# A decoder trunk on one core: two units side by side at the head, a pool window as a difference, no diagonals, a tail shared with GpSimd, and sine tables on GpSimd

## The chip, the cores and the metric

The kernel runs on one core of a Trainium2 chip. The metric is the device time of one execution in microseconds (us). Three runs of the kernel before gave 1794.53, 1795.22 and 1798.0 us, median 1795.22.

The engines go by the profile's names: PE is TensorE's matmul stream and PEld its weight load, DVE is VectorE, ACT is ScalarE, POOL is GpSimd, and SP issues most DMAs. Each engine works through its own instructions in the order in which they were written; a wait holds up everything behind it on that engine.

## The reference, cut to what matters

One layer, fp32, 2048 tokens of 1024 channels. Half of the projection `u` goes to a pooling mixer (four groups of 128 channels with windows 2, 4, 8, 16), half to a complex diagonal scan; both are joined by `w_out`, and a SwiGLU FFN with 2816 inner channels follows.

```python
def rmsnorm(x, g):
    y = xf * lax.rsqrt(jnp.mean(xf * xf, axis=-1, keepdims=True) + RMS_EPS)
    return y.astype(x.dtype) * g

# pool_mixer: for each window w
    mean = (c - lagged) / jnp.minimum(n_pos, float(w))[None, :, None]
    diffs.append(mean - ug[:, :, gi])
...
# ssm_mixer
    abar_r = mag * jnp.cos(li * dt)
    abar_i = mag * jnp.sin(li * dt)
    ...
    _, _, s_r, s_i = lax.associative_scan(_complex_affine_combine, (a_r, a_i, bu_r, bu_i), axis=1)
    y = ... + d_skip * ug
    y = jax.nn.gelu(y)
    y = y * jax.nn.sigmoid(y @ w_glu + b_glu)
...
        u = rmsnorm(h, norm_mix[i]) @ w_in[i]
        h = h + jnp.concatenate([y_pool, y_ssm], axis=-1) @ w_out[i]
        h = h + swiglu(rmsnorm(h, norm_ffn[i]), w_gate[i], w_up[i], w_down[i])
    return rmsnorm(h, norm_final)
```

## The kernel before, in words

**Matmuls.** Activations lie with 128 channels on the partitions and tokens along the free axis, in four token blocks of 512. A large fp32 matmul is done as three fp32r products of split operands: hi·hi, hi·lo, lo·hi. `split` (L335) makes the halves: ACT rounds the raw tile to hi (for x with the norm's gain `gmix` as scale), DVE subtracts it from the raw tile and so gets lo. One such product is a 128x512 matmul on PE; a unit of stage A is 24 of them (8 channel tiles times 3) for 128 output channels of one token block. The FFN saves products by a Strassen-like scheme that DVE's additions feed.

**Stages**, by the trace: the head and stage A to about 206 us (`phase_a`, first key 1 with the scan's four weight tiles m = 4 to 7, the token blocks in the order 3, 2, 1, 0; then key 2 with the pool's tiles); the eight lanes of the scan from about 133 to 337 us, PE being filled up beside them with the pool half of `w_out` (its partial sums go out through POOL's queue as `hp` and come back); GLU, the scan half of `w_out` and the second norm to 532 us; the FFN to 1526, its last down projection to 1777, and the tail, in which the last token block is done in two halves of 256 tokens (`c0` = 0 and 256).

**Norms.** Squares of a block are added up over the channel tiles, and a matmul with `mean` (128x1, each 1/1024) puts the means of 512 tokens as four columns into PSUM. `rsqrt_cols` (L358) takes the reciprocal root there in 13 small DVE instructions on the tile `nwt`. `rbank` (L390) makes four diagonal tiles with them (`ident` times a column of `rstd`, on DVE) and multiplies these by a tile of ones on PE, which lays rstd along the free axis over all partitions.

**The head.** `w_load(4)`, the gain vector and the four quarters of x (512 KB each) are loaded first, then w_in tiles 5, 6, 7. The first unit (m = 4) takes the quarters as they come; each `x_split` is followed by the squares of that quarter on ACT and their addition on DVE; tile 5 is split after the fourth quarter.

**Pool units.** `pool_unit` builds the window sum of 2, 4, 8 or 16 tokens by doubling, corrects the first tokens with `pin`, and subtracts w times u with a scalar_tensor_tensor of 1024 columns. There are two halves (1024 tokens each) for each of four windows.

**The scan.** For each lane s of 8, `ssm_table` (L717) forms cosine and sine tables from angle sums with six 128x512 tensor_tensors on DVE; `ssm_lane` then rotates the input, scans it (L886) and rotates it back, some 10 us of DVE. Table s+1 is formed while lane s runs. `ssm_build` clears a tile `T0` (L774, four times). The outputs of two lanes each are stored as `ys` with eight DMAs on POOL's queue.

**Order.** A planner writes the program out: class `Flow` keeps modelled clocks of the engines (`fl.t`, `fl.now`); generators registered as sides are resumed when their modelled inputs are due, or yield at `fl.when(...)`. So an edit to one instruction's engine or duration can shift what others are written before or after it.

**The tail.** Each output group of the last block is squared (ACT), added to one of two running sums (DVE), and the eighth square is given to the mean matmuls directly. When `rsqrt_cols` and `rbank` are through, groups k = 0 to 2 of each half are multiplied by rstd on POOL (`PK`; they were scaled with `gfin` on ACT before), the others on DVE with gfin in one scalar_tensor_tensor; SP stores the pairs.

## Time and profile before

| | |
|---|---|
| median of 3 runs | 1795.22 us (1794.53 to 1798.0) |
| the profiled execution | 1794.41 us, span 1792.5 us |
| PE busy | 1756.9 us, 98% of the span |
| DVE busy | 1343.6 us, 75% |
| ACT busy | 695.7 us, 39% |
| POOL busy | 164.9 us, 9% |
| mean granted TensorE clock | 0.994 |

The profile is of one execution. The span is the time from its first to its last recorded instruction or transfer; the execution's own time is 1.9 us longer. "Busy" counts every engine alone, so the columns overlap; 35.6 us of the span have no matmul. "Idle before" and the releaser after an arrow tell how long an engine stood before a row, and what it waited for last.

### The profile page before, as it was taken

To read this page: it belongs to the slowest core of one execution; us is meant where nothing else is said; L and a number is where in the kernel's file an instruction comes from. 1 tells how busy PE (TensorE), PEld (TensorE's weight loads), DVE (VectorE), ACT (ScalarE), POOL (GpSimd) and SP (SyncE) were. 2 spreads that over 40 slices of the span, in tenths; PEclk is the share of its full clock that TensorE was granted. 3 is DMA by queue.
4 is the path that set the end of the run, shared out by engine and by line. 5 is a ranking of instruction groups with operands and counts; after the bars stand their busy time and mean duration, and the time that the engine had idled before them with its cause. 6 is when DMAs were issued, how large, how long until landed. Compare 5 with 4: busy or idle time off the path is not lost.

```text
span 1792.5 us, 23179 instructions
## 1 busy us (share of the span) xinstructions
PE 1756.9 (98%) x8192; PEld 1441.7 (80%) x8192; DVE 1343.6 (75%) x2319; ACT 695.7 (39%) x1152; POOL 164.9 (9%) x311
## 2 busy tenths in 40 slices
PE   7999999999989999999999999999999999999997
PEld 5878777788868888888888888888888888888886
DVE  7879999657998777787788777776766556666666
ACT  5512223343353333333355333333334445354452
POOL 0000010100000121111101111211100000000001
PEclk9999999999999999999999999999999999999998
DMA  5462434684612255444364343454547665766752
GB/s 183 134 129 76 111 105 109 176 294 172 228 47 100 102 190 191 170 172 171 128 226 169 140 168 124 154 218 148 198 145 250 194 193 198 290 219 198 235 178 105
DMA packets 154596, 301.92 MB, mean 168 GB/s; under 512 B 25520, under 2 KB 49072, under 8 KB 154480
## 3 DMA queue, kind: packets, MB, share of 16 engines
q1 hardware_dynamic: 128912, 214.97, 37.7%
q0 software_dynamic: 25568, 85.48, 12.7%
q8 instruction: 64, 1.05, 0.2%
q14 instruction: 52, 0.43, 0.1%
HBM read 206.40 MB, written 92.80 MB: 167 GB/s over the span
## 4 chain that ended last, share of the span: by engine, by line
PE 89%; DVE 5%; issue 3%; DMA 2%; POOL 0%; ACT 0%; SPq 0%; DVEq 0%; POOLq 0%; ACTq 0%
PE p L207 89%; DVE s L184 3%; DMA s<-in_win_dram 1%; DVE s L195 1%; DVE t L184 1%; POOL ys L222 0%; DMA s<-ys 0%; DMA s<-in_cst_dram 0%; SPq L222 0%; DMA s<-in_wout_dram 0%; DMA ys<-b 0%; ACT s L203 0%; DVE b L184 0%; PE p L211 0%; DVE nwt L184 0%
## 5 line engine op out<-in xcount | busy, mean ns | idle before, releaser
L207 PE MATMUL p<-s,s 128*128 128x512 f32 (+3 forms) x4812 | 1200.9, 383 | 21.6 <-ACT s L203 11.1
L207 PEld LDWEIGHTS p<-s,s 128*128 128x128 f32 (+2 forms) x4812 | 849.1, 183 | 209.8 <-DVE s L184 14.0
L207 PE MATMUL p<-s,t 128*128 128x512 f32 (+2 forms) x1356 | 397.4, 383 | 0.7 <-DVE s L184 0.6
L207 PE MATMUL p<-s,b 128*128 128x512 f32 x1080 | 334.3, 389 | 0.0
L184 DVE TENSOR_TENSOR s<-s,s 128x512 f32<-128x512 f32 (+4 forms) x329 | 277.9, 868 | 64.5 <-ACT s L203 55.2
L207 PEld LDWEIGHTS p<-s,t 128*128 128x128 f32 x1356 | 249.7, 188 | 52.7 <-DVE s L184 1.8
L207 PEld LDWEIGHTS p<-s,b 128*128 128x128 f32 x1080 | 202.7, 188 | 42.0
L203 ACT ACTIVATE s<-s 128x512 fp32r<-128x512 f32 (+3 forms) x199 | 155.2, 792 | 111.5 <-DVE s L184 42.2
L203 ACT ACTIVATE s<-t 128x512 fp32r<-128x512 f32 (+1 forms) x186 | 113.7, 624 | 124.5 <-PE p L207 88.0
L184 DVE TENSOR_TENSOR s<-p,s 128x512 f32<-128x512 f32 (+3 forms) x185 | 116.8, 652 | 46.9 <-PE p L207 45.6
L203 ACT ACTIVATE t<-p 128x512 f32<-128x512 f32 (+1 forms) x107 | 63.5, 594 | 189.1 <-PE p L207 183.5
L203 ACT ACTIVATE t<-s 128x512 f32<-128x512 f32 (+2 forms) x126 | 76.6, 616 | 140.1 <-DVE s L184 112.1
L203 ACT ACTIVATE s<-p 128x512 f32<-128x512 f32 (+2 forms) x98 | 56.2, 590 | 168.5 <-PE p L207 142.1
L184 DVE TENSOR_TENSOR s<-t,s 128x512 fp32r<-128x512 f32 (+2 forms) x145 | 96.9, 678 | 27.4 <-issue 19.0
L207 PE MATMUL p<-b,s 128*128 128x512 f32 (+2 forms) x428 | 115.9, 389 | 0.7 <-DVE s L184 0.7
L184 DVE TENSOR_TENSOR t<-p,t 128x512 f32<-128x512 f32 x117 | 79.5, 688 | 34.4 <-PE p L207 31.9
L222 POOL DMA_DIRECT2D act_P<-t x81 | 43.8, 543 | 528.9 <-DVE t L184 528.4
L207 PEld LDWEIGHTS p<-b,s 128*128 128x128 f32 (+1 forms) x428 | 64.1, 172 | 21.0 <-issue 5.2
L184 DVE TENSOR_TENSOR s<-b,s 128x512 fp32r<-128x512 f32 (+1 forms) x89 | 60.9, 686 | 25.4 <-issue 12.1
L203 ACT ACTIVATE s<-b 128x512 fp32r<-128x512 f32 (+1 forms) x99 | 61.2, 622 | 47.3 <-PE p L207 25.5
L184 DVE TENSOR_TENSOR t<-t,t 128x512 f32<-128x512 f32 (+2 forms) x108 | 73.5, 681 | 5.6 <-ACT t L203 4.5
L184 DVE TENSOR_TENSOR s<-s,t 128x512 f32<-128x512 f32 (+1 forms) x77 | 52.9, 688 | 31.5 <-ACT t L203 30.4
(128 smaller groups left out, 1225.4 us busy)
## 6 DMA issues: line engine op xcount, KB each, us to landing
act_P<-t POOLq DMA_DIRECT2D x81, 256.0 KB, 4.9
s<-in_x_dram SPq DMA_DIRECT2D x40, 512.0 KB, 6.6
t<-ws_P SPq DMA_DIRECT2D x78, 256.0 KB, 2.7
t<-act_P SPq DMA_DIRECT2D x71, 256.0 KB, 3.1
b<-act_P SPq DMA_DIRECT2D x66, 256.0 KB, 3.0
s<-in_wu_dram SPq DMA_DIRECT2D x62, 256.0 KB, 5.3
s<-in_wd_dram SPq DMA_DIRECT2D x50, 256.0 KB, 5.3
t<-in_wd_dram SPq DMA_DIRECT2D x50, 256.0 KB, 3.2
```

What stands on the lines that cost most here:

```text
L184: self.eng(e).tensor_tensor(out, a, b, op=op)
L195: self.eng(e).scalar_tensor_tensor(out=out, in0=a, scalar=s, in1=b, op0=op0, op1=op1)
L203: self.nc.scalar.activation(out=out, in_=a, func=func, **kw)
L207: self.nc.tensor.matmul(out, l, r, start=start, stop=stop, skip_group_check=more)
L222: e.dma_start(dst, src)
```

## The change

Five edits, none of which changes what is computed.

1. Head. The first w_in tile is loaded in two halves with the first quarter of x (in two halves too) between them; tile 5 comes before the third and fourth quarters. `a_pair` does units m = 4 and 5 of the first block side by side, two quarters of one, two of the other, then in turn. Squares of that block are taken after all splits, and tile 6 is split before them.
2. The pool window of 2 is formed as a difference: the mean of two tokens minus the token itself is half of (previous minus this one), so the last subtraction with 1024 columns, and the `pin` correction, fall away for gi = 0.
3. Norms. `rbank` takes the column of rstd, broadcast over 128 columns, as one matmul operand and `ident` as the other; the four diagonals and the tile of ones are gone. EPS is put into PSUM by a matmul of `ident` with a small tile `eps`, and the Newton steps read PSUM, 11 DVE instructions instead of 13.
4. Tail. The first half's eight groups are all multiplied on POOL, of the second half k = 0 to 2 as before. Six squares are added up; the seventh and eighth go to the mean matmuls directly.
5. Scan. The six instructions of each `ssm_table` and the clearing of `T0` go from DVE to POOL.

```diff
@@ -25,6 +25,9 @@
+TE = 'g'
+DN = 6
+FN = 5.0
@@ -44,7 +47,7 @@
-PK = {3: 3, 2: 3}
+PK = {0: range(8), 256: range(3)}
@@ -360,37 +363,37 @@
+        mm(ps[:, js], ident, eps[:, js], True, False, 0.1)
         for i, s1 in enumerate(parts):
-            yield fl.when(s1) + SL
+            while callable(s1):
+                if s1():
+                    s1 = s1()
+                else:
+                    yield fl.now + 0.3
+            yield fl.when(s1) + (SL if c1 - c0 == 512 else 0.1)
...
-                mm(ps[:, j:j + 1], s1[:, j * 128:(j + 1) * 128], mean, i == 0 and j == js.start, i == len(parts) - 1 and j == js.stop - 1, 0.22)
+                mm(ps[:, j:j + 1], s1[:, j * 128:(j + 1) * 128], mean, False, i == len(parts) - 1 and j == js.stop - 1, 0.1)
...
-        a, y, h = (nwt[:, i, 0:n] for i in range(3))
-        ts("v", a, ps[:, js], EPS, None, ADD)
-        PS.free(ps)
-        ts("v", h.bitcast(I32), a.bitcast(I32), 1, None, ALU.logical_shift_right)
-        ts("v", a, a, -0.5, None, MUL)
+        y, h = (nwt[:, i, 0:n] for i in range(2))
+        ts("v", h.bitcast(I32), ps[:, js].bitcast(I32), 1, None, ALU.logical_shift_right)
...
-            tt("v", h, h, a, MUL)
+            stt("v", h, h, -0.5, ps[:, js], MUL, MUL)
...
+        PS.free(ps)
...
     def rbank(idx, c0=0, c1=512):
-        diag = T([128, 4, 128])
...
-        for j in js:
-            ts("v", diag[:, j, :], ident, rstd[:, idx, j:j + 1], None, MUL)
...
-            mm(ps[:, j * 128:(j + 1) * 128], ones, diag[:, j, :], True, True, 0.22)
-        T.free(diag)
+            mm(ps[:, j * 128:(j + 1) * 128], rstd[:, idx, j:j + 1].to_broadcast([128, 128]), ident, True, True, 0.22)
@@ -413,10 +416,12 @@
+        xhl[key, tb, q] = (hi, lo)
+        if key == 1 and not fl.now:
+            return raw
...
-        xhl[key, tb, q] = (hi, lo)
@@ -473,11 +478,33 @@
+    def a_pair(tb, ms, ps, half_way):
+        for n, (u, q) in enumerate(((0, 0), (0, 1), (1, 0), (1, 1), (0, 2), (1, 2), (0, 3), (1, 3))):
+            fl.until(lambda: ms[u] in whl)
+            hi, lo = whl[ms[u]]
+            xh, xl = xhl[1, tb, q]
+            for i in range(2):
+                k = 2 * q + i
+                mm(ps[u], hi[:, k, :], xh[:, i, :], k == 0, False)
+                mm(ps[u], hi[:, k, :], xl[:, i, :], False, False)
+                mm(ps[u], lo[:, k, :], xh[:, i, :], False, k == 7)
+            yield
+            if n == 3:
+                for h in half_way:
+                    h()
+
     def phase_a(key, ms, unit_done, hooks):
...
-            for mi, m in enumerate(ms):
+            units = list(enumerate(ms))
+            if key == 1 and n == 0:
+                ps = bank(), bank()
+                yield from a_pair(tb, ms, ps, hooks.pop((0, 1)))
+                for mi in range(2):
+                    unit_done(n, tb, mi, ps[mi])
+                units = units[2:]
+            for mi, m in units:
@@ -518,9 +545,18 @@
-        if half == 0:
-            tt("v", cur[:, :, 0:2], cur[:, :, 0:2], pin[:, gi], MUL)
-        stt("v", cur, u, -float(w), cur, MUL, ADD)
+        if gi:
+            if half == 0:
+                tt("v", cur[:, :, 0:2], cur[:, :, 0:2], pin[:, gi], MUL)
+            stt("v", cur, u, -float(w), cur, MUL, ADD)
+        else:
+            yield from room(1, 3)
+            cur, hl = S([128, 8, 128]), halo[:, 0, 0, 7:8]
+            tt("v", cur[:, 1:8, :], u[:, 0:7, :], u[:, 1:8, :], SUB)
+            tt("v", cur[:, 0, 1:128], u[:, 7, 0:127], u[:, 0, 1:128], SUB)
+            tt("v", cur[:, 0, 0:1], hl if half else u[:, 0, 0:1], u[:, 0, 0:1], SUB)
+            if half == 0:
+                cp("v", hl, u[:, 7, 127:128])
@@ -721,10 +757,10 @@
-            tt("v", t[:, i].rearrange("p q (m n) -> p q m n", n=16), x, wide(y[:, 1, qs], 3, sh), MUL)
+            tt(TE, t[:, i].rearrange("p q (m n) -> p q m n", n=16), x, wide(y[:, 1, qs], 3, sh), MUL)
...
-        tt("v", tab[:, 0], tab[:, 0], tmp[:, 0], SUB)
-        tt("v", tab[:, 1], tab[:, 1], tmp[:, 1], ADD)
+        tt(TE, tab[:, 0], tab[:, 0], tmp[:, 0], SUB)
+        tt(TE, tab[:, 1], tab[:, 1], tmp[:, 1], ADD)
@@ -771,8 +807,8 @@
-        nc.vector.memset(T0, 0.0)
-        fl.t["v"] += 0.6
+        nc.gpsimd.memset(T0, 0.0)
+        fl.t["g"] = max(fl.t["g"], fl.now) + 1.2
@@ -994,22 +1030,37 @@
-        w_load(4)
+        t0, w4 = ORD[1][0], S([128, 8, 128])
+        xr0 = xraw[1, t0, 0] = S([128, 2, 512])
...
-        for q in range(4):
-            x_load(1, ORD[1][0], q)
-        for m in (5, 6, 7):
+        load(w4[:, 0:4], win[4][:, 0:4, :])
+        for i in range(2):
+            load(xr0[:, i], x4[t0][:, i, :])
+        load(w4[:, 4:8], win[4][:, 4:8, :])
+        x_load(1, t0, 1)
+        w_load(5)
+        for q in (2, 3):
+            x_load(1, t0, q)
+        for m in (6, 7):
...
-        w_split(4, True)
+        whl[4] = (S([128, 8, 128], F32R), S([128, 8, 128], F32R))
+        raws = []
...
-            x_split(1, ORD[1][0], q)
-        st_side[ORD[1][0]] = fl.side(stats_x(ORD[1][0]), None)
-        fl.now += 7.0
-        w_split(5)
-        at(0, 1, w_split, 6)
+            if q < 2:
+                split(w4[:, 4 * q:4 * q + 4], *(t[:, 4 * q:4 * q + 4] for t in whl[4]))
+            elif q == 2:
+                S.free(w4)
+                w_split(5, True)
+            raws.append(x_split(1, t0, q))
+        w_split(6, True)
+        for q in range(4):
+            xacc[t0] = sq_add(xacc.get(t0), raws[q], q == 0)
+            S.free(raws[q])
+        st_side[t0] = fl.side(stats_x(t0), None)
+        fl.now += FN
@@ -1765,20 +1816,23 @@
-            if m < PK[tb]:
+            if not c0 or n <= DN:
...
+            if n > DN:
+                sums.setdefault((tb, c0, "p"), {})[n] = sq
+                return
...
-            elif n < 8:
+            else:
...
-            if n == 8:
-                while sums[tb, c0, "d"] < 8:
+            if n == DN:
+                while sums[tb, c0, "d"] < DN:
...
-                yield from last(tb, c0, c1, sq)
+                yield from last(tb, c0, c1)
...
         def down(hh):
@@ -1891,23 +1946,30 @@
+            mine = [k for k in range(8) if k in PK[c0]]
+
             def pooled():
-                for k in range(PK[tb]):
+                for k in mine:
...
-            for k in range(PK[tb], 8):
+            for k in range(8):
+                if k in mine:
+                    continue
...
-                stt("v", hk, hk, gfin[:, k:k + 1], ps[:, c0:c1], MUL, MUL)
+                if c0 and k >= DN:
+                    stt("v", hk, hk, gfin[:, k:k + 1], ps[:, c0:c1], MUL, MUL)
+                else:
+                    tt("v", hk, ps[:, c0:c1], hk, MUL)
...
-            T.free(r, sq)
+            T.free(r, *more.values())
@@ -1937,8 +1999,8 @@
-        nc.vector.memset(ones, 1.0)
...
+        nc.vector.memset(eps, EPS)
...
```

**Places in the order.** First SP's queue at the head: which loads are issued first. `s_1` is the first w_in tile, `in_x_dram` the quarters of x, each 512 KB at 128x1024. Before:

```order
L222 DMA s_1_338<-in_win_dram 128x1024
L222 DMA vec<-in_vecs_dram 128x64
L222 DMA s_2_341<-in_x_dram 128x1024
L222 DMA s_3_343<-in_x_dram 128x1024
L222 DMA s_4_345<-in_x_dram 128x1024
L222 DMA s_5_347<-in_x_dram 128x1024
L222 DMA s_6_349<-in_win_dram 128x1024
```

And in the changed kernel:

```order
L225 DMA vec<-in_vecs_dram 128x64
L225 DMA s_1_338<-in_win_dram 128x512
L225 DMA s_2_339<-in_x_dram 128x512 x2
L225 DMA s_1_338<-in_win_dram 128x512
L225 DMA s_3_345<-in_x_dram 128x1024
L225 DMA s_4_347<-in_win_dram 128x1024
L225 DMA s_5_349<-in_x_dram 128x1024
L225 DMA s_6_351<-in_x_dram 128x1024
```

The second w_in tile (`s_6_349` before, `s_4_347` after) has moved ahead of the third and fourth quarters of x. On PE the last products of the first unit before (`p_1`) are followed by the second unit (`p_3`), with the mean matmuls (`p_2`) after six of its products:

```order
L207 MATMUL p_1_402<-s_21_391,s_9_360 128x512
L207 MATMUL p_1_402<-s_20_390,s_10_361 128x512
L207 MATMUL p_3_438<-s_11_364,s_23_399 128x512
L207 MATMUL p_3_438<-s_12_365,s_23_399 128x512
L207 MATMUL p_3_438<-s_11_364,s_24_400 128x512
L207 MATMUL p_2_411<-mean,t_1_409 128x1 x4
L207 MATMUL p_3_438<-s_14_372,s_23_399 128x512
```

In the changed kernel `p_1` and `p_2` are the two units, `s_13`/`s_14` the second quarter of x, `s_15`/`s_16` tile 5, `s_17`/`s_18` the third quarter, and `p_3` takes the eps matmul:

```order
L210 MATMUL p_3_421<-eps,ident 128x4
L210 MATMUL p_1_411<-s_13_374,s_9_362 128x512
L210 MATMUL p_1_411<-s_14_375,s_9_362 128x512
...
L210 MATMUL p_1_411<-s_13_374,s_10_363 128x512
L210 MATMUL p_2_412<-s_11_366,s_15_380 128x512
L210 MATMUL p_2_412<-s_12_367,s_15_380 128x512
L210 MATMUL p_2_412<-s_11_366,s_16_381 128x512
```

The second unit's first half now stands after 12 products of the first unit, and needs tile 5 there; the mean matmuls stand behind the first two units and half of the third. On POOL, in the stretch of the last lanes, only stores stood before (`hp` partial sums, `ys_81` the outputs of the lanes 4 and 5):

```order
L222 DMA hp_2_105<-s_232_2757 128x1024
L222 DMA hp_3_106<-s_237_2800 128x1024
L222 DMA hp_0_107<-s_243_2865 128x1024
L222 DMA hp_1_108<-s_247_2934 128x1024
L222 DMA ys_81<-b_3_2219 16x8x256 x8
L222 DMA hp_2_109<-s_256_3017 128x1024
```

There stand now the tables of lane 6 (`s_247`, `s_248`) and lane 7 (`s_255` and on) between them:

```order
L225 DMA hp_2_105<-s_231_2700 128x1024
L225 DMA hp_3_106<-s_235_2738 128x1024
L187 TENSOR_TENSOR s_247_2891<-s_50_703 128x512
L187 TENSOR_TENSOR s_248_2892<-s_50_703 128x512
...
L187 TENSOR_TENSOR s_247_2891<-s_247_2891,s_248_2892 128x512 x2
L225 DMA hp_0_107<-s_244_2845 128x1024
L225 DMA ys_81<-b_3_2200 16x8x256 x8
L187 TENSOR_TENSOR s_255_3000<-s_50_703 128x512
```

So the table of lane 7 stands behind the eight stores of `ys_81`, which themselves wait for the GELU of lane 5's output.

## Rows read from the trace of the kernel before

**Rows 1.** The page's busy times, with the share of the span and the instructions.

```profile
PE 1756.9 (98%) x8192; PEld 1441.7 (80%) x8192; DVE 1343.6 (75%) x2319; ACT 695.7 (39%) x1152; POOL 164.9 (9%) x311
```

**Rows 2.** What PE waited for, over the whole span: engine, line and tile waited for, then us in total, times, longest.

```profile
PE p L207 <- ACT s L203: 11.1, 2, 9.3
PE p L207 <- DVE s L184: 10.8, 9, 3.3
```

**Rows 3.** Busy time by stretch: start:end of the stretch, its length, then busy us (and instructions) of PE, PEld, DVE, ACT, POOL, the granted clock, the DMA engines' share and GB/s.

```profile
142.00:206.00 64.00, 64.00 (x360) 50.63 (x357) 63.25 (x116) 18.47 (x27) 0.00 (x0) 1.00 0.25 84
206.00:302.00 96.00, 94.04 (x604) 72.36 (x600) 91.07 (x151) 26.48 (x46) 13.14 (x24) 1.00 0.50 115
302.00:350.00 48.00, 47.80 (x233) 36.35 (x234) 38.15 (x58) 15.04 (x25) 7.55 (x14) 1.00 0.48 139
360.00:471.00 111.00, 110.94 (x505) 92.36 (x506) 78.29 (x127) 41.80 (x58) 6.25 (x12) 1.00 0.64 228
471.00:532.00 61.00, 54.36 (x222) 42.86 (x221) 58.17 (x75) 28.62 (x42) 2.80 (x6) 0.94 0.33 121
532.00:1526.00 994.00, 994.00 (x4402) 823.52 (x4402) 720.59 (x1149) 394.70 (x675) 121.96 (x226) 1.00 0.49 169
```

**Rows 4.** The head in order of time (start, us, engine, line, operation, tiles, shape, count, and in brackets the idle time before it and its releaser). The row of 18 matmuls ends where the window was cut, at 27 us, with the second unit's last product.

```profile
8.48 1.34 ACT L203 ACTIVATE s<-s,vec 128x512 fp32r<-128x512 f32 x2 [3.27 <-DMA s<-in_x_dram]
9.26 5.42 PE L207 MATMUL p<-s,s 128*128 128x512 f32 x13 [9.26 <-ACT s L203]
14.11 1.41 DVE L195 SCALAR_TENSOR_TENSOR s<-s,vec,s 128x512 fp32r<-128x512 f32 x2
14.91 1.67 PE L207 MATMUL p<-s,s 128*128 128x512 f32 x6 [0.23 <-DVE s L195]
17.37 1.90 PE L207 MATMUL p<-s,s 128*128 128x512 f32 x7 [0.79 <-DVE s L195]
21.03 1.19 PE L207 MATMUL p<-s,s 128*128 128x512 f32 x4 [1.76 <-DVE s L184]
21.25 1.04 ACT L203 ACTIVATE s<-s 128x1024 f32<-128x1024 f32 x1
22.05 0.95 PE L207 MATMUL p<-mean,t 128*128 128x1 f32 x8
22.86 4.39 PE L207 MATMUL p<-s,s 128*128 128x512 f32 x18
```

**Rows 5.** What the DMA engines moved in the first 18 us, in 40 equal slices (0.45 us each).

```profile
GB/s 0 0 0 0 182 346 391 331 306 273 246 173 319 319 291 264 319 373 355 310 310 382 401 401 437 410 428 428 419 382 417 422 418 419 410 391 372 314 287 181
```

**Rows 6.** DVE in order of time around the last tables: lane 6 begins at 311.88, the table of lane 7 (six instructions) at 322.15, the scan of lane 7 at 329.97; then, from the groups of 142 to 206 us, the pool's subtraction and the clearing of T0 (count, busy us, mean ns).

```profile
311.88 2.47 DVE L184 TENSOR_TENSOR s<-p,s 128x512 f32<-128x512 f32 x4
322.15 2.49 DVE L184 TENSOR_TENSOR s<-s 128x512 f32<-128x512 f32 x4
324.55 1.28 DVE L184 TENSOR_TENSOR s<-s,s 128x512 f32<-128x512 f32 x2
329.97 2.43 DVE L886 TENSOR_TENSOR_SCAN s<-rho,s 128x256 f32<-128x256 f32 x4
...
L195 DVE SCALAR_TENSOR_TENSOR s<-s,s 128x1024 f32<-128x1024 f32 x4 | 4.9, 1225 | 0.1
L774 DVE MEMSET s<- 128x1024 f32 x1 | 0.9, 912 | 0.2 <-issue 0.2
```

**Rows 7.** POOL in order of time: the stores of `ys` around 320 us, and the multiplications of the tail, first and second half.

```profile
319.47 1.20 POOL L222 DMA_DIRECT2D ys<-b  x2 [0.45 <-ACT b L203]
321.10 3.62 POOL L222 DMA_DIRECT2D ys<-b  x6 [0.43 <-issue]
1777.46 2.57 POOL L184 TENSOR_TENSOR s<-s,t 128x256 f32<-128x256 f32 x3 [15.05 <-ACT t L203]
1785.28 2.10 POOL L184 TENSOR_TENSOR s<-s,t 128x256 f32<-128x256 f32 x3 [5.25 <-ACT t L203]
```

**Rows 8.** DVE beside POOL in the tail: an addition of 256 columns before POOL starts and one beside its first instructions; two of the Newton steps; the six multiplications of the second half.

```profile
1776.48 0.41 DVE L184 TENSOR_TENSOR b<-b,t 128x256 f32<-128x256 f32 x1
1778.20 0.56 DVE L184 TENSOR_TENSOR b<-b,t 128x256 f32<-128x256 f32 x1
1780.92 0.37 DVE L189 TENSOR_SCALAR nwt<-nwt 128x2 int32<-128x2 int32 x2
1785.23 2.44 DVE L195 SCALAR_TENSOR_TENSOR s<-s,vec,p 128x256 f32<-128x256 f32 x6 [0.82 <-ACT t L203]
```

**Rows 9.** PE in order of time in the middle of the program: the rows before which it stood.

```profile
231.84 1.30 PE L207 MATMUL p<-b,s 128*128 128x256 f32 x4 [0.71 <-DVE s L184]
234.83 1.16 PE L207 MATMUL p<-s,t 128*128 128x128 f32 x8 [0.63 <-DVE s L184]
302.20 8.21 PE L207 MATMUL p<-s,s 128*128 128x512 f32 x35 [0.82 <-DVE s L184]
509.06 11.38 PE L207 MATMUL p<-s,s 128*128 128x512 f32 x36 [3.29 <-DVE s L184]
```

**Rows 10.** DVE in order of time where the second norm's last needed block is finished: the diagonals, and the first multiplication by the bank that PE makes of them.

```profile
468.74 0.86 DVE L189 TENSOR_SCALAR t<-ident,rstd 128x128 f32<-128x128 f32 x4
471.30 2.72 DVE L195 SCALAR_TENSOR_TENSOR s<-s,vec,p 128x512 f32<-128x512 f32 x4 [0.50 <-PE p L207]
```

More of the change, by code (lines that the diff above doesn't have):

```diff
@@ L307, in hybrid_kernel @@
     ident = cpool.tile([128, 128], F32, name="ident")
-    ones = cpool.tile([128, 128], F32, name="ones")
     mean = cpool.tile([128, 1], F32, name="mean")
+    eps = cpool.tile([128, 4], F32, name="eps")
     vec = cpool.tile([128, 64], F32, name="vec")
@@ L502, in pool_unit @@
         cur, prev = u, None
-        for l in range(gi + 1):
+        for l in range(gi + 1 if gi else 0):
             s = 1 << l
@@ L1880, in final, with last @@
             T.free(r)
-        def last(tb, c0, c1, sq):
-            yield from rsqrt_cols(sums[tb] + [sq], 8 + tb, c0, c1, True)
+        def last(tb, c0, c1):
+            more = sums.setdefault((tb, c0, "p"), {})
+            yield from rsqrt_cols(sums[tb] + [lambda n=n: more.get(n) for n in range(DN + 1, 9)], 8 + tb, c0, c1, True)
             ps = yield from rbank(8 + tb, c0, c1)
```

## The prediction, made before the changed kernel had run

> **What bounds the kernel now.** I read the busy times first: PE works 1756.9 of 1792.5 us [rows 1], so all that is not PE work is 35.6 us. An edit on another engine can only win where PE stands, and an edit that adds matmuls costs nearly their length. The waits of PE say where it stands: 11.1 us on ACT, 9.3 of them the first wait of the program, and 10.8 us on DVE in nine waits [rows 2]. The stretches tell the rest [rows 3]. From 142 to 302 us DVE is as good as full (63.25 of 64, 91.07 of 96) and PE nevertheless nearly full; from 360 to 471 us DVE has 33 us to spare; from 471 to 532 DVE is full again (58.17 of 61) and PE loses 6.6 us plus a stretch at a lower granted clock (0.94 there as a mean); the FFN from 532 on has no gap at all, so no edit can win there. Its pitch, 994 us for 4402 matmuls, is 0.226 us at the full clock.
>
> So four places count: the head, the waits on DVE around 230 and 302 us, the waits after 505 us, and the tail. All sums are made against the profiled execution, 1794.41 us; the median of the runs stands 0.8 us above it, and I add that at the end.
>
> **Head.** In the first 13 us or so a matmul takes 5.42 / 13 = 0.42 us, half speed [rows 4]. PE starts at 9.26, runs 13, 6, 7 and 4 matmuls with 2.8 us of waits for the splits on DVE, then the eight mean rows (22.05 to 22.86), then 18: the 48 products of the units 4 and 5 end at 22.86 + 18 x 0.226 = 26.93, or 26.1 without the mean rows, which come later after the change. What limits it is that every quarter of x feeds only six matmuls (1.4 us), while a quarter costs 1.41 us of DVE for its lo parts plus 1.2 us for adding up the squares [rows 4]. After the change the squares come later, and each quarter feeds twelve. Tile 5 is the fourth half megabyte instead of the sixth. The first 8.4 us bring tile 4 and the first quarter [rows 4], and from there DMA moves some 300 to 430 GB/s [rows 5], say 1.3 us per 512 KB: the second quarter lands at 9.7, tile 5 at 11.0. ACT rounds it in 1.04 [rows 4] and DVE makes lo in 1.22, as for other instructions of 1024 columns [rows 6]: ready at 13.3. Until then PE does unit 4's twelve products at 0.42 us, 8.5 to 13.5. The third and fourth quarters land at 12.3 and 13.6 and are split by 16.4, before PE needs them (24 products after 13.5). So 36 x 0.226 = 8.1 us follow without a wait: 21.6. The gain is 26.1 - 21.6 = 4.5 us. I take off 0.4 us for tile 7, whose lo now stands on DVE behind the squares and the next block's splits (about 28.3 us, while PE could use it at 27.9). Value 4.1. Bounds: if PE stays at half speed for 15 more matmuls, 3 us are lost, gain 1; at best 5.5.
>
> **Norms.** The eps matmuls: eleven with four columns and, in the tail, two with two. No such matmul is in the trace; the nearest are the mean matmuls, two rows each, eight rows in 22.86 - 22.05 = 0.81 us [rows 4], so 0.2 us each. Eleven on a full PE cost 2.2 us. From both sides: 0.1 and 0.3 each, 1.1 to 3.3. The bank matmuls keep their count; a weight load from a broadcast column is new, and I leave it at the price of the old one, between nothing and 0.1 us each way for 32 of them that are not in the tail: plus or minus 3 us.
>
> The diagonals and two Newton steps leave DVE: 0.86 us for four diagonals [rows 10], 0.37 for two steps [rows 8], 1.2 us per bank. In most banks PE has other work meanwhile and nothing is won. The one that counts is the bank of 468.74 to 471.30 [rows 10]: it opens the stretch in which DVE is full and PE waits, so what it comes sooner PE waits less: 1.2 us. Bounds 0 (if the rows between take its place) and 9.8 (all of that stretch's loss, in a rival below).
>
> **Pool, tables, T0.** A table costs DVE 2.49 + 1.28, begun at 322.15 and over at 325.8: 3.6 us by start times [rows 6]. Seven of the eight lie between 142 and 350 us: 25 us. The pool difference saves 1.22 us and a small correction twice, 2.6 us; three clearings of T0 0.91 each, 2.7 us [rows 6]. Together DVE loses 30 us of work in a stretch of 208 us in which it had 15.5 us idle [rows 3]. PE does not gain 30 us by it, because it is full too: it has waits for DVE of 0.71 + 0.63 + 0.82 = 2.2 us there [rows 9]. I take two thirds of these as gone, 1.4 us; bounds 2.2 gained and the loss of the first rival.
>
> What POOL pays: the trace has no table instruction on POOL. Its multiplications of 256 columns take 2.10 / 3 = 0.70 us, and 0.86 while DVE adds from SBUF beside them [rows 7]; DVE itself goes from 0.41 for 256 columns [rows 8] to about 0.62 per start for 512 [rows 6]. So a table instruction of 512 columns costs POOL between 1.1 (grown like DVE's) and 1.7 us (twice 0.86); I take 1.4, twice the undisturbed row. A table is then 8.4 us beside a lane of DVE of 10.3 us (311.88 to 322.15 [rows 6]), so POOL can keep up. DVE beside POOL: an addition of 0.41 took 0.56 [rows 8], 0.15 us more per POOL instruction of 0.7, or 21% of POOL's time. For 42 instructions, 59 us, DVE loses 12.6 us, less than the 30 that it gains.
>
> By the Trainium skill, "SBUF — State Buffer", section "SBUF: two separate sides", the shared ports are an exclusive lock, held by whichever of a GpSimd instruction that reads SBUF and a DVE instruction with two SBUF inputs starts first, and the other blocks fully. The two rows of the tail show a slowdown of both engines, but not a full block: 0.15 us beside instructions of 0.70 to 0.86. By the rule to the full the time would be the first rival's.
>
> **Tail.** POOL's eight multiplications of the first half begin where its three began, 1777.46, and at 0.70 to 0.86 end between 1783.1 and 1784.3; then three of the second half, until 1785.2 to 1786.9. Before, POOL ended at 1787.38 [rows 7] and DVE at 1787.67 [rows 8]. The second half's rstd comes sooner by two diagonals (0.43), two Newton steps (0.37) and the additions of the last two squares, later by the eps matmul and four more mean matmuls at half speed, partly while PE waits anyway: about 0.7 us sooner. DVE then has five multiplications instead of six, 0.4 us less. If both count it is 1.1 sooner, if POOL's queue decides 0.5. I take 0.5; bounds -0.5 (POOL at its slowest rate throughout and its last pair's store behind it) and 1.5.
>
> **Sum.** 1794.4 - 4.1 + 2.2 - 1.2 - 1.4 - 0.5 = 1789.4; with the 0.8 of the median 1790.2. I predict 1790.
>
> **Rivals.**
>
> *The ports make the lanes late.* If every POOL instruction of the tables blocks DVE for its whole length, DVE loses 59 us and gains 30: 29 more than before, of which 15.5 fit into its idle time, and 13.5 us come out on PE, since lane 7's output is late and the fillers run out. 1790.2 + 1.4 + 13.5 = 1805. It decides from the point where DVE loses more than 30 + 15.5 = 46 us, 78% of POOL's time. Against it stands the 21% of the tail's rows; for it, that in the lanes nearly all DVE instructions read two SBUF tiles. Chance 0.12.
>
> *POOL's queue makes the last lane late.* The table of lane 7 stands behind eight stores of lane 5's output, which wait for a GELU, took 1.20 + 3.62 us and ended at 324.7 [rows 7]; with 8.4 us of table behind them lane 7 would start at 333 where DVE had its table at 325.8 [rows 6]. If the lanes come 3 us sooner by the relief, 4 us are left, and PE has few fillers then: 1794. For it speaks the order of the stores; against it that the whole chain moves up with DVE. Chance 0.20.
>
> *The head does not come sooner.* If the smaller loads land no sooner, or the lower clock lasts through the second unit, 1 us is won instead of 4.1: 1793. The clock's part cannot be read from before, since PE had waits all through. Chance 0.14.
>
> *The backlog at 471 us goes.* If DVE arrives there ahead, the waits of 505 us (3.29 [rows 9]) and the others, 6.6 in all, and the 36 matmuls that took 11.38 instead of 8.1 us [rows 9], 9.8 us together, are saved instead of 1.2: 1790.2 - 8.6 = 1782. For it: DVE is relieved before; against it: DVE already had 33 us idle between 360 and 471 [rows 3], so earlier relief does not carry over. Chance 0.10.
>
> **How the numbers follow.** My forecast has 0.42, the rivals 0.56, and 0.02 is left for an order by the planner that helps or harms as a whole. Within 0.2% (3.6 us, about what a measurement of this kernel can tell from no change) means 1791.6 to 1798.8. The forecast's own range is 1786 to 1794, by the bounds on the head and the bank's weight load; five parts in six of it lie below 1791.6 (0.35). The backlog gives 0.10 more, and a quarter each of the queue's and the head's cases 0.08: faster 0.53. Slower are most of the ports' case (0.11), a sixth of the queue's (0.04) and 0.02 of the rest: 0.17. The same: 0.30. The range that leaves out two in ten runs from the backlog's 1783 to 1801, which cuts the upper half of the ports' case.
>
> **What would show it.** Right: PE's twelfth product over at about 13.5 and the two units at about 21.6, with no wait between; eps rows of 0.1 us; DVE with clear idle time between 206 and 302; POOL table rows near 1.4 us and DVE rows beside them little longer than 0.68; PE full to 350; the wait of 3.3 us after 505 at about 2; POOL's eleven multiplications over by 1787. Wrong: a PE wait between 300 and 350 released by POOL or by a lane behind a late table (queue); DVE rows of 1 us or more beside POOL (ports); no lost time at 498 to 531 (backlog); matmuls of 0.42 us past 15 us (head).

## The result, and the profile after

The changed kernel takes 1808.95 us (median of four runs, 1807.58 to 1810.01); the kernel before, on the same chip, 1795.79. The ratio is 1.0073, 95% interval 1.0055 to 1.0091: slower by 13 us, where I had forecast 1790, in a range from 1783 to 1801. The profiled execution is one of 1807.58 us.

The busy times, which answer to [rows 1], and what PE waited for, [rows 2]:

```profile
PE 1763.6 (98%) x8226; PEld 1447.9 (80%) x8226; DVE 1324.6 (73%) x2184; ACT 702.2 (39%) x1160; POOL 234.6 (13%) x368
```

```profile
PE p L210 <- ACT s L206: 17.3, 4, 8.2
PE p L210 <- DVE s L187: 11.1, 7, 4.2
PE p L210 <- DVE rstd L198: 4.2, 1, 4.2
```

DVE has 135 instructions fewer and only 19 us less busy time: what is left of them takes longer. The waits of PE on ACT are 6 us more. The stretches, columns as in [rows 3], show where:

```profile
142.00:206.00 64.00, 64.00 (x308) 49.83 (x307) 59.38 (x102) 17.16 (x25) 8.92 (x6) 1.00 0.22 71
206.00:302.00 96.00, 89.99 (x571) 70.75 (x569) 86.55 (x118) 24.39 (x42) 47.62 (x50) 0.98 0.45 113
302.00:350.00 48.00, 41.44 (x192) 30.13 (x192) 30.78 (x48) 12.59 (x21) 13.10 (x18) 0.86 0.40 116
```

PE lacks 6.0 us before 302 and 6.6 behind it, and its granted clock is 0.86 in the last stretch (it is at 1.2 GHz from 298 to 315 us, in the two waits shown next and behind them). POOL went from 13 to 48 us there. In order of time, PE, ACT, DVE and POOL around that wait:

```profile
304.31 0.80 PE L210 MATMUL p<-s,s 128*128 128x512 f32 x1 [8.24 <-ACT s L206]
309.36 5.06 PE L210 MATMUL p<-s,s 128*128 128x512 f32 x11 [4.25 <-DVE s L187]
...
303.21 1.06 ACT L206 ACTIVATE s<-s 128x1024 fp32r<-128x1024 f32 x1 [7.75 <-DVE s L187]
...
295.21 7.89 DVE L187 TENSOR_TENSOR s<-s 128x896 f32<-128x896 f32 x2
...
295.43 4.08 POOL L187 TENSOR_TENSOR s<-s 128x512 f32<-128x512 f32 x4
299.48 2.47 POOL L187 TENSOR_TENSOR s<-s,s 128x512 f32<-128x512 f32 x2
```

The page of the profile names ACT, but ACT had waited 7.75 us for DVE. There, two instructions of 896 and 127 columns take 7.89 us instead of 1.3, with no wait of their own; they end 1.2 us after the last of the six table instructions on POOL (299.48 + 2.47 = 301.95). Then 11 matmuls take 5.06 us, twice their time. Earlier, tables and DVE alternate:

```profile
218.46 6.28 DVE L187 TENSOR_TENSOR s<-s,s 128x512 f32<-128x512 f32 x6
...
220.01 5.64 POOL L187 TENSOR_TENSOR s<-s 128x512 f32<-128x512 f32 x4 [2.44 <-PE p L210]
```

Three of these six DVE instructions overlap POOL's and take 1.54 us each instead of 0.68; three of POOL's four take 1.50 instead of the 1.06 that they need alone. The groups of DVE from 206 to 350 us (count, busy, mean ns) say the same:

```profile
L187 DVE TENSOR_TENSOR s<-s,s 128x512 f32<-128x512 f32 x26 | 19.9, 817 | 0.0
...
L187 DVE TENSOR_TENSOR s<-p,s 128x512 f32<-128x512 f32 x20 | 12.7, 685 | 25.2 <-POOL s L187 14.1 <-PE p L210 11.1
L187 DVE TENSOR_TENSOR s<-s 128x896 f32<-128x896 f32 x4 | 10.9, 2737 | 0.0
```

With both inputs in SBUF the mean rises from 0.68 to 0.82, with one in PSUM (`p,s`) it stays. That is not for want of meeting POOL: 19 DVE instructions with an input in PSUM ran beside a table instruction and none was held, of 33 without one 26 were. The idle time before the `p,s` group is new: 14.1 us in which DVE waited for a table. Adding up, over all DVE instructions that took at least 0.15 us more than the median of their shape, what they took beyond it gives 28.1 us of excess before the tail and 1.9 in it; the same sum in the trace of before is 0.0. The table instructions on POOL beside which they fall (count, busy, mean ns, idle time before and its releasers):

```profile
L187 POOL TENSOR_TENSOR s<-s 128x512 f32<-128x512 f32 x32 | 41.1, 1310 | 87.8 <-DVE s L198 54.4 <-DMA s<-s 19.6 <-PE p L210 9.9
L187 POOL TENSOR_TENSOR s<-s,s 128x512 f32<-128x512 f32 x16 | 22.2, 1409 | 0.0
```

### The profile page after: what moved, and what is told of

Its sections match the earlier page's. It is cut to its first block, busy times and chain, and to the rows that moved or that the text cites. A ratio compares the mean times of both kernels' runs of the same rounds, so it can differ in the third digit from the quotient of the medians.

```text
span 1805.8 us, 23246 instructions
## 1 busy us (share of the span) xinstructions
PE 1763.6 (98%) x8226; PEld 1447.9 (80%) x8226; DVE 1324.6 (73%) x2184; ACT 702.2 (39%) x1160; POOL 234.6 (13%) x368
## 3 DMA queue, kind: packets, MB, share of 16 engines
q0 software_dynamic: 25568, 85.48, 12.6%
## 4 chain that ended last, share of the span: by engine, by line
PE 82%; DVE 7%; issue 7%; DMA 2%; POOL 2%; ACT 1%; SPq 0%; POOLq 0%; DVEq 0%; ACTq 0%
PE p L210 82%; DVE s L187 4%; DVE t L187 1%; POOL s L187 1%; DVE s L198 1%; ACT s L206 0%; DMA s<-in_x_dram 0%; SPq L225 0%; DMA hp<-s 0%; DMA b<-us 0%; DMA s<-s 0%; DMA s<-in_wout_dram 0%; POOL ys L225 0%; DVE nwt L198 0%; DMA us<-t 0%
## 5 line engine op out<-in xcount | busy, mean ns | idle before, releaser
L210 PE MATMUL p<-s,s 128*128 128x512 f32 (+3 forms) x4008 | 1004.3, 383 | 28.2 <-ACT s L206 17.3
L210 PEld LDWEIGHTS p<-s,s 128*128 128x128 f32 (+2 forms) x4008 | 700.2, 183 | 186.4 <-ACT s L206 18.6
L210 PE MATMUL p<-s,b 128*128 128x512 f32 x1468 | 438.2, 389 | 0.0
L210 PE MATMUL p<-s,t 128*128 128x512 f32 (+1 forms) x1280 | 371.1, 383 | 0.0
L210 PEld LDWEIGHTS p<-s,b 128*128 128x128 f32 x1468 | 275.4, 188 | 56.8
L210 PE MATMUL p<-b,s 128*128 128x512 f32 (+2 forms) x672 | 186.2, 391 | 1.0 <-DMA s<-s 1.0
L206 ACT ACTIVATE t<-s 128x512 fp32r<-128x512 f32 (+2 forms) x141 | 85.8, 617 | 148.1 <-DVE s L187 130.1
L206 ACT ACTIVATE t<-p 128x512 f32<-128x512 f32 x100 | 59.6, 596 | 189.4 <-PE p L210 186.6
L187 DVE TENSOR_TENSOR s<-s,t 128x512 f32<-128x512 f32 (+2 forms) x104 | 70.2, 676 | 25.7 <-ACT t L206 24.8
L206 ACT ACTIVATE b<-s 128x512 fp32r<-128x512 f32 (+1 forms) x109 | 67.5, 624 | 38.4 <-DVE s L187 25.1
```

Of the source, the lines that this page charges most:

```text
L187: self.eng(e).tensor_tensor(out, a, b, op=op)
L206: self.nc.scalar.activation(out=out, in_=a, func=func, **kw)
L210: self.nc.tensor.matmul(out, l, r, start=start, stop=stop, skip_group_check=more)
```

## The experiments

Sixteen kernels. In the expectations P is the theory of the ports, Q that of late tables, R any other edit or the order, T1 and T2 the two for the tail, S starvation, D and W the two for the losses of single edits. The ratios compare each run with the kernel before on the same chip; where two runs from different chips are compared by their medians, a difference of 2 or 3 us is weak evidence.

**Tables back on DVE.**

```diff
-TE = 'g'
+TE = 'v'
```

> The changed kernel with the six instructions of each sine table back on DVE (T0's clearing stays on POOL, all other edits stay). Theory P (ports: DVE instructions with two SBUF operands are held by POOL's table instructions, one of them for 7.7 us, and the lane and PE come late by it) and theory Q (queue: the tables are formed late because POOL needs 6 to 12 us for each and has stores ahead of them): the waits of 8.2 and 4.3 us and the matmuls at half speed behind them go, some 15 us, time 1791 to 1795, no DVE instruction much longer than its usual time outside the tail. Theory R (another edit, or the planner's new order, costs the time): 1803 or more, PE still stands about 12 us around 300.

1790.82 us (10 runs), ratio to before 0.9974, interval 0.9963 to 0.9985; span 1788.0, 17.8 less than after. R falls, so far as another edit is meant; moving the tables also changes the order that the planner writes, so the run with subtractions below keeps the order of this one. The waits near 300 are gone and no DVE instruction outside the tail is longer than usual; the same two stretches:

```profile
206.00:302.00 96.00, 95.58 (x600) 75.28 (x597) 92.82 (x153) 27.26 (x46) 14.16 (x25) 1.00 0.46 113
302.00:350.00 48.00, 47.80 (x240) 35.25 (x239) 29.23 (x44) 14.27 (x23) 7.03 (x13) 1.00 0.59 159
```

**Three multiplications of the first half on POOL, as before.**

```diff
-PK = {0: range(8), 256: range(3)}
+PK = {0: range(3), 256: range(3)}
```

> The changed kernel with only three multiplications of the first half on POOL, as before, in the tail; all else stays. Theory T1 (POOL's eight multiplications hold up the Newton steps of the second half, 4.0 us instead of the 2.0 that 11 undisturbed steps take): the steps take 2.0 to 2.4 us, the time from the second half's first mean matmul to the end of the span falls from 15.8 to about 13.8 us, the whole is 1.5 to 2.5 us shorter. Theory T2 (the four more mean matmuls and the eps matmul lengthen the chain): the steps still end as late as before, the whole changes by less than 0.7 us.

> Tables back on DVE and three multiplications of the first half on POOL, the other edits stay. By P or Q with T1: 1789 to 1793, 1.5 to 2.5 us below the run with the tables alone; by R 1801 or more.

One run of the first gave 1805.61 us; the second, with the tables on DVE too, 1791.0 (0.9974, 0.9964 to 0.9984), no different from the tables alone. Half of T1 holds: the steps get shorter, the time does not. In the changed kernel the Newton steps beside POOL's row of seven take up to four times their 0.16 us, and the bank's matmuls wait 4.22 us for rstd:

```profile
1790.87 4.80 POOL L187 TENSOR_TENSOR s<-s,s 128x256 f32<-128x256 f32 x7 [15.48 <-ACT s L206]
...
1792.42 0.55 DVE L194 TENSOR_SCALAR nwt<-nwt 128x2 int32<-128x2 int32 x1
1793.01 0.64 DVE L187 TENSOR_TENSOR nwt<-nwt 128x2 f32<-128x2 f32 x1
...
1796.42 1.19 PE L210 MATMUL p<-ident,rstd 128*128 128x128 f32 x4 [4.22 <-DVE rstd L198]
```

With three on POOL (the run with both) a step takes 0.16 and that wait is 2.29, but DVE now has five multiplications of the first half more. Two of them stand before an addition that the mean matmuls need, and the first of these waits 1.81 us for ACT, so the mean matmuls wait 2.20 us:

```profile
1775.75 0.76 DVE L187 TENSOR_TENSOR s<-p,s 128x256 f32<-128x256 f32 x2 [1.81 <-ACT s L206]
...
1776.89 0.61 PE L210 MATMUL p<-mean,s 128*128 128x1 f32 x4 [2.20 <-DVE s L187]
...
1781.55 1.19 PE L210 MATMUL p<-ident,rstd 128*128 128x128 f32 x4 [2.29 <-DVE rstd L198]
```

So POOL's help in the tail is paid back on DVE: from the end of the last product to the end of the span it is 16.97 us before, 16.62 after, 16.67 and 16.05 in these two, and 16.60 with the tables alone on DVE. The half microsecond between the last and the third of these does not show in the runs (1791.0 against 1790.82).

**Only the tables, on POOL, in the kernel before.** In `ssm_table`, the rest as before:

```diff
-            tt("v", t[:, i].rearrange("p q (m n) -> p q m n", n=16), x, wide(y[:, 1, qs], 3, sh), MUL)
+            tt("g", t[:, i].rearrange("p q (m n) -> p q m n", n=16), x, wide(y[:, 1, qs], 3, sh), MUL)
...
-        tt("v", tab[:, 0], tab[:, 0], tmp[:, 0], SUB)
-        tt("v", tab[:, 1], tab[:, 1], tmp[:, 1], ADD)
+        tt("g", tab[:, 0], tab[:, 0], tmp[:, 0], SUB)
+        tt("g", tab[:, 1], tab[:, 1], tmp[:, 1], ADD)
```

> The kernel before with nothing but the six instructions of each table on POOL. By P or Q: slower than before by 10 to 18 us, 1806 to 1814, with DVE instructions of twice their time beside POOL's, 25 to 35 us of such excess in all. By R: 1793 to 1799.

1820.54 us, ratio 1.0133 (1.0104 to 1.0162): 25 us slower, more than expected. The excess is 29.9 us, in 36 instructions of which none takes 3 us; between 100 and 350 us PE waits at six places, three of them:

```profile
220.44 1.52 PE L207 MATMUL p<-b,s 128*64 128x256 f32 x12 [1.96 <-DVE s L184]
244.54 1.22 PE L207 MATMUL p<-b,s 128*128 128x256 f32 x2 [4.45 <-DVE s L184]
...
324.53 2.50 PE L207 MATMUL p<-s,s 128*128 128x512 f32 x5 [4.83 <-DVE s L184]
```

**POOL works, but nobody waits for it.** The kernel with tables on DVE, with a small tile `scr` of 192 columns, and at the place of each table:

```diff
+        for i in range(14):
+            nc.gpsimd.tensor_tensor(scr, scr, scr, op=SUB)
```

> The kernel with the tables back on DVE (1790.8 us), and beside it POOL does work that nobody waits for: at the place of each table fourteen subtractions of 192 columns of a small tile from itself, about 60 us in all, in program order on POOL's queue alone; every other engine has the same instructions in the same order. Theory P (POOL instructions that read SBUF hold up DVE instructions by themselves): DVE shows 20 us or more of excess over the usual times, and the time rises by 8 us or more, to 1799 or above. Theory Q (what costs is that lanes wait for tables that POOL forms late): no table is late here, the time stays within 3 us of 1790.8; the stores behind the subtractions come some us later and cost nothing.

and with thirty memsets of the tile in their place:

```diff
+        for i in range(30):
+            nc.gpsimd.memset(scr, 0.0)
```

> The same with thirty memsets of 192 columns at each place instead of the subtractions: POOL is about as long busy and its stores wait as long, but it reads no SBUF. P: no excess on DVE, time within 2 us of 1790.8. If POOL's business as such or its stores' lateness costs: as far above 1790.8 as the run with the subtractions.

The subtractions: 1814.08 us (ratio to before 1.0107, 1.0089 to 1.0125), 23 above the kernel without them; the memsets 1793.0 (0.9991, 0.9982 to 1.0001), 2 above it. The excess on DVE before the tail is 20 us with the subtractions, none with the memsets. POOL's groups of both:

```profile
L763 POOL TENSOR_TENSOR scr<-scr 128x192 f32<-128x192 f32 x112 | 92.3, 824 | 8.3
```

```profile
L763 POOL MEMSET scr<- 128x192 f32 x240 | 62.2, 259 | 13.4
```

Four DVE instructions in order of time beside the subtractions, and four of the same kind beside memsets:

```profile
337.96 3.72 DVE L187 TENSOR_TENSOR s<-s 128x512 f32<-128x512 f32 x4
```

```profile
281.90 2.49 DVE L187 TENSOR_TENSOR s<-s 128x512 f32<-128x512 f32 x4
```

They are 3.72 us against 2.49. The run with subtractions decides: no table is late, every other engine has the same instructions in the same order as with the tables on DVE, and 20 us of excess cost 23 us of time. A POOL that only writes costs 2 us, about one wait of PE (2.86 us near 297, 0.42 with no memsets). The memsets kept POOL busy for less time (62 us against 92), so they are not quite the same burden, but the stores behind them came as late: in either run DVE waits once for an `hp` store of POOL's queue, first with the subtractions, then with the memsets:

```profile
300.75 1.89 DVE L187 TENSOR_TENSOR s<-p,s 128x512 f32<-128x512 f32 x3 [1.94 <-DMA hp<-s]
```

```profile
290.66 1.89 DVE L187 TENSOR_TENSOR s<-p,s 128x512 f32<-128x512 f32 x3 [2.06 <-DMA hp<-s]
```

So late stores cost about the 2 us, and a loss of this size needs no late table. P explains it without Q; that late tables add nothing in the changed kernel is not shown by this.

**Breaks in the row of six.** In the changed kernel a memset of `scr` between any two instructions of a table:

```diff
             tt(TE, t[:, i].rearrange("p q (m n) -> p q m n", n=16), x, wide(y[:, 1, qs], 3, sh), MUL)
+            nc.gpsimd.memset(scr, 0.0)
...
         tt(TE, tab[:, 0], tab[:, 0], tmp[:, 0], SUB)
+        nc.gpsimd.memset(scr, 0.0)
```

> The changed kernel (tables on POOL) with a memset of 192 columns between any two of a table's six instructions, on POOL alone. Theory S (the DVE instruction of 7.7 us is starved because POOL takes the ports again before DVE gets its turn; the memsets give it a turn): no DVE instruction beside a table takes more than 3 us, the waits of 8.2 and 4.3 us near 300 shrink to under 4 us together, time 1796 to 1802. Rival: the wait near 300 comes from the sum of late lanes and stays, time 1807 or more, since POOL needs 1.3 us more per table.

1807.54 us (1.0073, 1.0056 to 1.0091): nothing won. S is right in its first clause (no DVE instruction beside a table takes more than 2.1 us) and wrong in the second; the rival forecast the time. DVE and PE in order of time:

```profile
296.44 3.11 DVE L187 TENSOR_TENSOR s<-s 128x896 f32<-128x896 f32 x2
...
299.54 5.07 DVE L925 TENSOR_TENSOR_SCAN s<-rho,s 128x256 f32<-128x256 f32 x4
...
300.76 0.80 PE L210 MATMUL p<-s,s 128*128 128x512 f32 x1 [3.45 <-ACT s L206]
309.33 2.93 PE L210 MATMUL p<-s,s 128*128 128x512 f32 x6 [7.77 <-DVE s L187]
```

The starved instruction is through in 2.05 us, but now the scans behind it take 1.3 each instead of 0.67, and PE waits 3.45 + 7.77 in place of 8.24 + 4.25. The excess is 23.9 us, not much below the 28.1 without the breaks: the waiting is spread over more instructions, and DVE comes out about as late.

**EPS without the matmul.** Tables on DVE, and in `rsqrt_cols`:

```diff
-        mm(ps[:, js], ident, eps[:, js], True, False, 0.1)
...
+        ts("v", a, ps[:, js], EPS, None, ADD)
...
-            stt("v", h, h, -0.5, ps[:, js], MUL, MUL)
+            stt("v", h, h, -0.5, a, MUL, MUL)
```

> The kernel with the tables back on DVE, and EPS added by a DVE instruction on the four columns as before the change instead of by the matmul; the Newton steps read that tile (12 DVE instructions). If the eps matmuls cost what I took (0.2 us each on a full PE, 11 of them): 2 us faster than 1790.8, 1788 to 1789.5. Rival: they lie in waits or cost less than 0.1 us: within 0.7 us of 1790.8.

1788.55 us (0.9966, 0.9955 to 0.9977), 2.3 below the tables on DVE alone by the medians, as expected; by the ratios to before, each on its own chip, it is 1.4 and the intervals overlap. The two profiled spans (1788.2 and 1788.0) do not show it, so a gain is likely and its size open.

**One edit at a time, in the kernel before.** The lines of the diff above for the head (`a_pair` and the new order of loads and splits); for the norms (`rsqrt_cols`, `rbank`); for the pool window and T0 (`pool_unit`, `ssm_build`); and the first and last of these together:

> The kernel before with the new head alone (order of the loads, two units side by side, squares after the splits). If the head is worth what I worked out: 4.1 us, in a range of 1 to 5.5, so 1790 to 1794 beside 1795.4; PE's first 48 products over between 21.6 and 23 us instead of 26.9, and the mean matmuls of the later blocks earlier by the same. Rival: the gain is lost again before 350 us, within 1 us of before.

> The kernel before with the new norms alone (no diagonals, bank by a broadcast column, eps by a matmul, 11 steps). By my sum: 11 eps matmuls cost 2.2 us, the stretch from 471 us wins 1.2, the tail's chain 0.7: 0.3 us slower, 1794 to 1797. Rival: DVE's shorter chain before 471 us wins nothing since other DVE work takes its place: 1 to 2 us slower.

> The kernel before with the pool window of 2 as a difference and T0 cleared on POOL, nothing else. By my sum PE wins at most a part of its 2.2 us of waits for DVE between 230 and 302: 0 to 1 us faster, 1794 to 1796; the memsets on POOL hold up no DVE instruction.

> The kernel before with the new head, the pool difference and T0 on POOL; norms, tail and tables as before. Theory D (to about 350 us DVE sets the end of the lanes; what PE wins at the head is kept only if the last lane's scan does not come later than about 330, and the pool difference and T0 take 4 us of work from DVE before it): last scan at 328 to 333, no PE wait above 3 us between 300 and 350, time 1790 to 1794. Rival W (which versions lose 7 to 12 us near 320 to 345 is decided by the order that the planner happens to write, not by DVE's work): last scan at 335 or later and 1798 or more, as with the head alone.

The head alone: 1802.82 us (1.0039, 1.0024 to 1.0054). The norms alone: 1803.88 (1.0046, 1.003 to 1.0062). Pool and T0: 1796.83 (1.0004, 0.9992 to 1.0016), no change. Head, pool and T0: 1799.82 (1.0022, 1.0012 to 1.0031). Of the four only pool and T0 came as expected; in the fourth W's time came, its scan missed by 0.7 us. The head alone does win at the head: PE works 135.7 of the first 142 us, 130.0 before. The gain is lost, and more with it, where the last lanes feed PE, with waits of 2.4, 5.9 and 3.2 us and matmuls at 1.2 GHz behind them:

```profile
329.61 2.08 PE L210 MATMUL p<-s,s 64*128 64x256 f32 x8 [5.90 <-DVE s L187]
...
344.07 1.82 PE L210 MATMUL p<-s,s 64*128 64x256 f32 x8 [3.16 <-DVE s L187]
```

The last lane's scan starts at 337.3 there, at 330.0 before ([rows 6] names it), at 335.4 with the norms alone and 334.3 in the fourth. DVE has worked 298.1 us by then in the kernel before, 299.1 with the head, 294.3 with the norms and 293.9 in the fourth: not the amount but the idle time between grew, 32 to 38, 41 and 40 us. Theory D falls: its cause is not the amount of DVE's work.

**All but the head, tables on DVE.**

> All edits but the new head, tables on DVE: norms, pool difference, T0 on POOL, tail. Theory D: DVE has less work before the last scan than with the norms alone, so that scan comes at 328 to 332 and the head's 4 us are missing: 1794 to 1797. Rival W: the last scan at 335 or later and 1800 or more, as with the norms alone.

1798.59 us (1.0013, 1.0000 to 1.0026), ten runs from 1792 to 1803; last scan at 336.0. Neither D's time nor W's. Beside the run with tables on DVE (1790.82, ratio 0.9974), which has the new head too, the head is worth some 7 us in this company; alone it cost 6.4.

**The order alone.** The constant by which the planner moves its clock after the head is 4 higher, in the kernel before and in the one with tables on DVE; instructions the same, their order not:

```diff
-        fl.now += 7.0
+        fl.now += 11.0
```

```diff
-FN = 5.0
+FN = 9.0
```

> The kernel before with the same instructions, but written out in another order: the constant by which the planner moves its own clock after the head is 11 instead of 7. Theory W (small differences of the order in which the lanes' work is written are worth several us by themselves): the time differs from before by 3 us or more, with the loss or gain at the PE waits between 200 and 350 us and the last lane's scan moved by as much. Rival: within 2 us of before, and the losses of the head alone and the norms alone are those edits' own.

> The changed kernel with tables on DVE (1790.8 us) and that constant at 9 instead of 5, nothing else. W: 3 us or more away from 1790.8, more likely slower, 1794 or above, with a wait of PE near 290 to 345. Rival: 1789 to 1793.

1794.81 us (0.9994, 0.9984 to 1.0004) and 1793.98 (0.9988, 0.9978 to 0.9999): none in the first; in the second 3.2 us by the medians, 2.5 by the ratios, with intervals that overlap. So this shift of the order is worth some 3 us, if anything. Whether another order can cost the 6 to 8 us of the head and the norms alone is not shown, and why these two lose that much stays open.

**The version that the runs point to.** Tables on DVE, EPS on DVE, three multiplications on POOL in the first half.

> The version that the runs point to: the changed kernel with tables on DVE, EPS added on DVE instead of by a matmul, and three multiplications of the first half on POOL. Expected at 1788 to 1789, 0.3 to 0.6 us below the run without the eps matmul (the tail after the last product takes 16.1 to 16.5 instead of 16.9 us), some 7 us faster than the kernel before and 20 faster than the changed one.

1789.21 us (0.9963, 0.995 to 0.9976): 7 us below before and 20 below the changed kernel, and not to be told from the run without the eps matmul (1788.55), so the 0.3 to 0.6 us expected of the tail are not shown. Either beats both kernels.

## Why the prediction was wrong, point by point

**The step that failed** is the price of DVE beside POOL: "an addition of 0.41 took 0.56 [rows 8], 0.15 us more per POOL instruction of 0.7, or 21% of POOL's time", 12.6 us of loss against 30 of relief. The term of the sum that stands on it, 1.4 us won by pool, tables and T0, was a loss of 18 (1808.95 us with the tables on POOL, 1790.82 with them on DVE). Measured are 28.1 us of excess beside 63 us of table instructions (41.1 for 32 and 22.2 for 16), 44% of POOL's time. A single DVE instruction that met the end of a POOL instruction is no rate: POOL's first multiplication ran from 1777.46 to 1778.48, and this addition began 0.28 us before its end. Another addition of two SBUF tiles, at 1777.48, lay wholly beside that multiplication and took its usual 0.41; there it was POOL that took 1.02 instead of 0.70. DVE's neighbours in the tail mostly read PSUM, those in the lanes mostly two SBUF tiles; the prediction noted that against itself and still took the tail's rate. The mechanism was the first rival's (1805 us, chance 0.12), but not its threshold: I let it decide only from 46 us of loss, as if DVE's 15.5 us of idle time could take up a loss anywhere. 28 us were enough, because they fell on instructions that PE waited for: the one of 7.7 us stands right before both waits near 300. The 14 us in which DVE waited for tables add little that can be seen: 9.8 of them come at 336, behind these waits, with PE full to 360.

The Trainium skill's rule ("SBUF — State Buffer", section "SBUF: two separate sides") says what happens: an exclusive lock between a GpSimd instruction that reads SBUF and a DVE instruction with two SBUF inputs. The trace agrees in three places: 1.54 against 0.68 us with two SBUF inputs, 0.685 with one in PSUM, and no excess beside memsets, which read nothing. The section has the side that comes second wait for the whole instruction of the other; it does not speak of a wait through several, and here one lasts 7.7 us through a row of six.

**What POOL pays** came out right, in part by luck: 1.4 us taken per table instruction as the undisturbed price, means of 1.35 and 1.43 measured between 100 and 350 us. Undisturbed they take 1.06 and 1.28; the rest is POOL being held by DVE, which the sum had not put in.

**The queue's rival** shows on DVE and not on PE: the table of lane 7 stood behind the eight stores, ended at 337, and DVE waited 9.8 us for it, while PE was full from 314 to 360.

**Head.** It wins at the head (PE has worked 92.7 of the first 100 us, 88.0 before), and is sized 1 us too high:

```profile
5.99 3.29 PE L210 MATMUL p<-s,s 128*128 128x512 f32 x6 [5.99 <-ACT s L206]
9.08 0.42 PE L210 MATMUL p<-eps,ident 128*128 128x4 f32 x2
10.85 14.60 PE L210 MATMUL p<-s,s 128*128 128x512 f32 x54 [1.35 <-ACT s L206]
25.29 0.95 PE L210 MATMUL p<-mean,t 128*128 128x1 f32 x8
```

PE starts at 5.99, not 8.5, then waits 1.35 us for the second half of tile 4 and the second quarter; 60 products are through at 25.29, the first 48 so at 25.29 - 12 x 0.226 = 22.6 (21.6 predicted, 26.1 before without the mean rows): 3.5 us won instead of 4.5. PE started 2.5 us sooner than I had taken, but stood again, and 14 products ran at half speed instead of 12. The 1.2 us that I took for adding up the squares stand in no line of [rows 4]; the trace has 1.23 at 12.96 us. The stall for tile 7 did not come. That the gain lasts to the end was not argued, only assumed: alone it was lost by 345 us.

**Norms.** The eps matmuls, 2.2 us by my sum, take less by the trace: each is two rows of PE, and from the first row's start to the next matmul's the ten that follow the one above take 1.6 us in all. The runs (2.3 us by the medians, 1.4 by the ratios) do not settle it. The broadcast weight load costs nothing that shows: four bank matmuls take 1.19 us in the tail, at half speed, as they did before. The gain of 1.2 us in the stretch from 471 us did not come to that; shifted by the 13 us that the kernel is late, it reads

```profile
484.00:545.00 61.00, 54.76 (x223) 43.49 (x222) 59.77 (x78) 31.17 (x46) 3.19 (x6) 0.94 0.32 117
```

against 54.36 [rows 3]: 0.4. DVE is as full as before, other work fills the place. **Pool and T0**: no gain alone, within the 0 to 1 us expected. **Tail**: 0.5 predicted, 0.35 measured, near it by luck: the Newton steps took 4.0 us, since POOL held them up, instead of the 2.1 that they take with three multiplications on POOL.

**The sum without the tables** was 1790.2 and the run without them gave 1790.8. After the single runs that is an agreement of totals only: the same edits one by one gave +6.4, +7.5 and +0.4 us.

## What to carry to other kernels

Work moved from DVE to GpSimd to relieve DVE relieved nothing here, where both read SBUF: price it at first as if the two shared one engine (here eight tables of 3.6 us taken away, 29 us, and 28 given back), and look first at whether the DVE work beside it has an operand in PSUM. With a DVE that is 95% full in front of a PE that is 98% full, a gain upstream lasted only up to the next place where PE waits for DVE; the head cost 6.4 us alone and won some 7 in company, so measure edits together as well as alone. A contention can be told from a late result by giving the other engine idle work of the same size that nobody waits for.

## What the runs showed of the hardware that I had not expected

A DVE instruction can be held through six GpSimd instructions (7.7 us) rather than one, in this kernel and again in the run with three multiplications in the tail; with memsets between the six it is held for one only. POOL can be held as long: beside the subtractions one of POOL's four here takes 5.6 us instead of 0.5, through seven DVE instructions with two SBUF inputs that take their usual time:

```profile
108.33 7.38 POOL L763 TENSOR_TENSOR scr<-scr 128x192 f32<-128x192 f32 x4
109.35 1.20 DVE L187 TENSOR_TENSOR s<-s,s 128x1024 fp32r<-128x1024 f32 x1
110.48 2.48 DVE L187 TENSOR_TENSOR s<-s 128x512 f32<-128x512 f32 x4
112.89 1.27 DVE L187 TENSOR_TENSOR s<-s,s 128x512 f32<-128x512 f32 x2
```

Small DVE instructions suffer most, against their own length: a Newton step of 0.16 us took up to 1.2 beside a table in the kernel before with tables on POOL. It holds too for a copy and a tensor_scalar with one SBUF input there (1.21 us, and 1.95 for two, instead of 0.17 each). By the Trainium skill, "SBUF — State Buffer", section "Who interferes with whom", such instructions can enter a two-port mode and then contend as well; these rows agree that they contend, the mode is not seen in them. Where the two alternate, both lose: 1.50 us instead of 1.06 per table instruction on POOL, as shown above.
